# Attention with two accumulator banks, three banks for two units' scores, and a gate part moved ahead of the sample's

## The chip, the core and the metric

The kernel runs on one core of a Trainium2 chip. The metric is the device time of one launch in microseconds (us). The core's engines are TensorE (PE, with weight loads as PEld), VectorE (DVE), ScalarE (ACT), GpSimd (POOL) and SyncE (SP), which issues nearly all DMAs. TensorE writes its results to PSUM, which has eight banks of 512 float32 columns on 128 partitions.

## The reference

One layer step for a prompt of 2048 rows and a sample of 32 rows, each of 1024 columns:

```
z = rms_norm(x) @ w_in                       # 1024 -> 3072, split in six parts of 512
xl, gl, q, k, v, ga = split(z)
q, k = rms_norm per head (8 heads of 64)
lru = rg_lru(causal_conv(xl))                # gated linear recurrence over the rows
att = softmax(q k / 8 + bias[rel]) v         # each chunk of 64 rows reads itself and 8 chunks back
mix = concat(lru * silu(gl), att * silu(ga)) @ w_out
h   = x + mix
y   = h + (p @ w_pe) * sigmoid(rms_norm(h) @ w_pg)
```

The sample attends to 512 cached rows and its own 32. The outputs are y for prompt and sample, and the new states. Values are kept as pairs of float16 halves (high and low part), so one product of two matrices is three products of halves.

## The kernel before, in words

The rows are worked on in 16 tiles of 128 (tiles 0 to 15), and the sample is a seventeenth. A first stage, up to about 650 us, makes the projections and the recurrence and stores q, k, v and the gate path to memory. The second stage is attention, output projection and output gate, and the change lies there.

*Attention.* A tile is cut into units: one head each (eight to a tile; tile 1 has two heads in each of four units; the sample has four heads in each of two). Per unit, in this order:

- `u_scores`: TensorE multiplies q with two to ten blocks of keys (line L977, two matmuls of 128 columns for each block of 128 keys, ten matmuls for a unit from tile 4 on) into a score tile in PSUM, `pss`. VectorE adds the bias, takes the row's maximum and writes to SBUF (L988), and forms the exponent's offset (L991). ScalarE takes the exponential (L994).
- `u_split`, called after the next unit's scores: the high half is made by ScalarE (L1009, even units) or GpSimd (L1007, odd units), the low half by VectorE (L1010); both stand in `Phl`, of which there are three. SyncE issues a transposing DMA into `PT` (L1012), of which there are four.
- `u_pv`, five units later (`LAG`): TensorE multiplies the transposed probabilities with the values (L1032, 15 matmuls of 64 columns for a unit from tile 4 on) into the tile's accumulator in PSUM, `pso`.

After a tile's last unit `a_out` divides the accumulator by the sums into SBUF (VectorE, L1068), GpSimd multiplies with the gate path `ga` (L1069, which frees the buffer for the next `ga` load at L928), and `halves` splits and transposes the result (`An`, `AT`).

*Output.* `o_out` has four products of 12 matmuls for a tile into PSUM tiles `psu` (`L` is the recurrence's half, `AT` the attention's), each added to h by VectorE (L1112), and then a normalisation: ScalarE L1116, GpSimd L95 and L96, ScalarE L160, VectorE L163 writes `hn`, and SyncE transposes it to `hT` (L1121). `o_gate` multiplies `hT` with the gate's weights (`psg`, 24 matmuls) and p's halves with theirs (`pse`, 6), ScalarE (L1145, L1146) and VectorE (L1147) combine them, GpSimd (VectorE for tile 15) adds h (L1148), and SyncE stores (L1149). Tile 15's gate is cut into 512, 256 and 256 columns; others have two parts of 512. `o_load` loads the next tile's rows and transposes p (`pn`, `pT`). `psu`, `psg` and `pse` share three PSUM banks.

*Order.* A generator `fill` gives out the output work in portions: within a tile's time of eight units it alternates between the four products of one tile and the gate of the tile before it, one or two portions for each unit. For the sample it has its own list of portions. The program's text thus gives a priority, `flush_pv` (value product and `a_out`) gets a higher one, and a planner lays out each engine's queue ahead of time from its own estimates: it takes the work that it believes to be ready, in the order of priority. On the chip each queue runs in the order laid out, and waits at what is not there yet. The planner also places the semaphore waits, from which tile each instruction reads and writes.

*PSUM.* In this stage the scores have two tiles of 640 columns, each padded to two whole banks, the accumulator has one bank, and the output work three.

```
ps_s = pool("ps_s", bufs=2, space=PSUM)
ps_o = pool("ps_o", bufs=1, space=PSUM)
...
ps = ps_s.tile([128, 640], F32, tag="s", name="pss")
...
acc[i] = ps_o.tile([128, 512], F32, tag="o", name="pso")
```

Of the kernel before, what the change touches and what calls it, by code (L numbers as in the profile page):

```python
# [8 lines left out]
F32 = mybir.dt.float32  # L9
# [6 lines left out]
PSUM = bass.MemoryType.PSUM  # L16
# [18 lines left out]
def hybrid_layer(  # L35
# [853 lines left out]
    ch = pool("ch")  # L889
    ao = pool("ao")  # L890
    ol = pool("ol")
    ps_s = pool("ps_s", bufs=2, space=PSUM)
    ps_o = pool("ps_o", bufs=1, space=PSUM)
    units, acc, sums = {}, {}, {}
    kv, qT, sgT, nkv = {}, {}, {}, [0]

# [68 lines left out]
    def u_scores(i, u):  # L965

        ks = keys_of(i)
        ps = ps_s.tile([128, 640], F32, tag="s", name="pss")
        q = qT[i]
        parts, W, WP = unit_parts(i, u)  # L970
        for together in [parts] if i == SAMPLE else [[p] for p in parts]:
            for j, (key, n) in enumerate(ks):
                k = k_of(key)
                for a in range(2):
                    for h, R, rw, c0 in together:
                        c = slice(c0 + j * 128, c0 + j * 128 + n)
                        last_mm[0] = nc.tensor.matmul(ps[rw, c], lhsT=q[:, h % 2, a * 4 + h // 2, :R], rhs=k[:, h, :n],  # L977
                                         start=a == 0, stop=a == 1)
        m = 1 if i == SAMPLE else len(parts)
        mx = sm.tile([128, m], F32, tag=f"mx{m}", name="mx", bufs=3)  # L980
        if i == SAMPLE:
            S = biasS[u]
            nc.vector.scalar_tensor_tensor(S[:, :W], ps[:, :W], ratS, S[:, :W], op0=OP.mult, op1=OP.add)
            nc.vector.tensor_reduce(mx, S[:, :W], axis=AX.X, op=OP.max)
        else:
            S = T("S", [128, 640], F32, 3, ch)
            for j, (h, _, _, c0) in enumerate(parts):
                nc.vector.tensor_tensor_reduce(out=S[:, c0:c0 + W], in0=ps[:, c0:c0 + W], in1=bias[:, h, 640 - W:],  # L988
                                               op0=OP.add, op1=OP.max, scale=1.0, scalar=-3e38, accum_out=mx[:, j:j + 1])
        nb = sm.tile([128, m], F32, tag=f"nb{m}", name="nb", bufs=3)  # L990
        nc.vector.tensor_scalar(nb, mx, nscP, LN1024, op0=OP.mult, op1=OP.add)  # L991
        for j in range(m):
            e, c0 = (u, 0) if i == SAMPLE else parts[j][0::3]
            nc.scalar.activation(S[:, c0:c0 + W], S[:, c0:c0 + W], AF.Exp, bias=nb[:, j:j + 1], scale=scP,  # L994
                                 accum_out=sums[i][:, e:e + 1])
        units[i, u] = S
# [158 lines left out]
    def fill():  # L1155
        prev = iter(())
        for n, i in enumerate(order):
            o = o_out(i)
            if i == SAMPLE:

                for g, k in ((o, 4), (prev, 2), (o_gate(i), 4), (o, 1), (prev, 9)):
                    for _ in range(k):
                        if next(g, 0) != 0:
                            yield
                break
            for which in (0, 0, 1, 0, 1, 0, 1, 1):
                next(prev if which else o, None)
                yield
                if which == 0 and n + 1 < len(order) and S["o", i].get("hT") is None and not S.get(("o", order[n + 1])):
                    o_load(order[n + 1])  # L1170
            next(o, None)
            prev = o_gate(i)
        yield
# [15 lines left out]
    for n, (i, u) in enumerate(slots):  # L1189
# [14 lines left out]
        elif fl is None:  # L1204
            esr.close()
            wgp, ot = pool("wgp", side="right"), pool("ot", side="right")
            ps = pool("ps", bufs=3, space=PSUM, side="right")
# [93 lines left out]
```

## Time and profile before

| | |
|---|---|
| median of 3 runs | 1235.5 us (1233.63 to 1238.19) |
| the profiled execution | 1231.86 us, its span 1229.9 us |
| granted TensorE clock, mean | 0.947 |
| TensorE busy | 1078.4 us, 88% of the span |
| VectorE busy | 850.8 us, 69% |
| ScalarE busy | 591.3 us, 48% |
| GpSimd busy | 430.5 us, 35% |

The page that comes with a run shows one profiled execution. Times are counted from the span's start. A row of a group of instructions or of the timeline names line, engine, operation, what is written and read (out<-in) and how many instructions; in brackets stands the idle time of the engine before it and what ended that wait. Matmuls are pipelined, so those of one group overlap, and an engine whose queue stands still counts as idle.

### The profile page before, as it was taken

Reading aid. Unit: us, or ns where it says so; the run is one execution under the profiler, and the core shown is the slowest. Engines: PE = TensorE matmul, PEld = TensorE weight load, DVE = VectorE, ACT = ScalarE, POOL = GpSimd, SP = SyncE. Lnnn points to the kernel's source line nnn. Section 1 sums busy time; section 2 is a strip of 40 time slices with the busy share of each in tenths; the row PEclk is TensorE's granted clock in tenths of the full one; section 3 lists DMA queues with packets and bytes.
Section 4 is the critical chain, followed back from the end, with each engine's and each line's share of the span. In section 5 each row is a group of like instructions: output and inputs, shape, how many; then the busy total and the mean of one; then the engine's idle time right before and its main releaser. Section 6 shows DMA issues by size and latency. Waiting matters only on the chain. (4 is left out here: it accounts for less than half of the span.)

```text
span 1229.9 us, 22389 instructions
## 1 busy us (share of the span) xinstructions
PE 1078.4 (88%) x8395; PEld 626.2 (51%) x8395; DVE 850.8 (69%) x1932; ACT 591.3 (48%) x1040; POOL 430.5 (35%) x482
## 2 busy tenths in 40 slices
PE   3779997997697988788988699999999999999896
PEld 1335664653364654565644355555555555555443
DVE  5997557666885676877855676677777777677544
ACT  6542374544636746247654344444445444545223
POOL 3875123444542437452421222222222222222221
PEclk9789998998898998899899699999999999999998
DMA  8785225994856476540498987999989998998841
GB/s 288 212 216 159 75 67 143 263 253 127 228 159 172 143 204 180 167 107 22 146 338 262 239 156 162 171 207 194 191 186 198 181 196 190 185 200 188 187 84 26
DMA packets 357725, 217.47 MB, mean 177 GB/s; under 512 B 296032, under 2 KB 298632, under 8 KB 357488
## 3 DMA queue, kind: packets, MB, share of 16 engines
q1 hardware_dynamic: 357184, 215.50, 72.0%
q8 instruction: 65, 1.06, 0.4%
q10 hardware_dynamic: 432, 0.54, 0.1%
q14 instruction: 44, 0.36, 0.1%
HBM read 98.87 MB, written 46.76 MB: 118 GB/s over the span
## 5 line engine op out<-in xcount | busy, mean ns | idle before, releaser
L183 PE MATMUL psp<-wA,xT 128*128 128x512 f16 x1536 | 368.3, 400 | 30.1 <-ACT sq L656 9.9
L183 PEld LDWEIGHTS <-xT 128*128 128x128 f16 x1536 | 155.9, 102 | 264.2 <-issue 82.0
L994 ACT ACTIVATE S<-S,nb,s 128x640 f32<-128x640 f32 (+5 forms) x130 | 110.5, 850 | 221.4 <-DVE nb L991 211.8
L183 PE MATMUL psg<-g,hT 128*128 128x512 f16 (+1 forms) x792 | 179.8, 376 | 4.4 <-DMA hT<-hn 2.7
L587 PE MATMUL psx<-xT,wl 128*128 128x256 f16 x1536 | 178.7, 276 | 0.0
L587 PEld LDWEIGHTS <-wl 128*128 128x128 f16 x1728 | 157.3, 99 | 25.6 <-issue 2.1
L1010 DVE TENSOR_TENSOR Phl<-S,Phl 128x640 f16<-128x640 f32 (+4 forms) x126 | 96.9, 773 | 89.4 <-POOL Phl L1007 52.7
L1032 PE MATMUL pso<-kv,PT 128*128 128x64 f16 (+1 forms) x1704 | 116.9, 195 | 25.6 <-DMA PT<-Phl 13.2
L1032 PEld LDWEIGHTS <-PT 128*128 128x128 f16 (+2 forms) x1800 | 109.7, 99 | 47.5 <-issue 16.8
L1007 POOL TENSOR_SCALAR Phl<-S 128x640 f16<-128x640 f32 (+4 forms) x63 | 49.1, 779 | 213.7 <-ACT S L994 179.8
L183 PEld LDWEIGHTS <-hT 128*128 128x128 f16 x792 | 73.6, 98 | 79.8 <-DMA hT<-hn 3.4
L977 PE MATMUL pss<-kv,qT 128*128 128x128 f16 (+2 forms) x1200 | 107.0, 221 | 6.3 <-DVE mx L988 4.4
L977 PEld LDWEIGHTS <-qT 128*128 128x128 f16 (+1 forms) x1200 | 93.9, 99 | 19.6 <-issue 6.2
L988 DVE CUSTOM_DVE_ANT_0 S<-pss,bias 128x640 f32<-128x640 f32 (+4 forms) x128 | 93.0, 731 | 2.5 <-PE pss L977 2.0
L183 PE MATMUL psu<-o,AT 128*128 128x512 f16 x384 | 91.8, 390 | 1.3 <-DMA AT<-An 1.3
L183 PE MATMUL psu<-o,L 128*128 128x512 f16 x384 | 88.0, 379 | 0.0
L1148 POOL TENSOR_TENSOR gt<-gt,h 128x512 f32<-128x512 f32 (+1 forms) x32 | 41.7, 1304 | 60.7 <-DVE gt L1147 56.4
L95 POOL TENSOR_SCALAR fh<-ssqh,e 128x8 f32<-128x8 f32 (+1 forms) x34 | 17.5, 514 | 126.4 <-DVE ssqh L282 99.8
L96 POOL TENSOR_TENSOR fh<-fh,pw 128x8 f32<-128x8 f32 (+1 forms) x34 | 61.0, 1793 | 1.6
L183 PEld LDWEIGHTS <-AT 128*128 128x128 f16 x384 | 36.6, 101 | 43.5 <-issue 5.7
L183 PEld LDWEIGHTS <-L 128*128 128x128 f16 x384 | 35.6, 98 | 38.5
L90 PE MATMUL psm<-dg,ones 128*128 128x128 bf16 x25 | 6.0, 241 | 55.7 <-DVE dg L87 29.7
(284 smaller groups left out, 1693.5 us busy)
## 6 DMA issues: line engine op xcount, KB each, us to landing
stw<-in_w_in_dram SPq DMA_DIRECT2D x20, 512.0 KB, 7.1
x<-in_x_prompt_dram SPq DMA_DIRECT2D x16, 512.0 KB, 4.8
stg<-in_w_out_dram SPq DMA_DIRECT2D x16, 512.0 KB, 5.1
stg<-in_w_ple_gate_dram SPq DMA_DIRECT2D x16, 512.0 KB, 4.8
qT<-qd SPq DMA_DIRECT2D x32, 256.0 KB, 5.4
kv<-kvd SPq DMA_DIRECT2D x16, 512.0 KB, 4.1
h<-in_x_prompt_dram SPq DMA_DIRECT2D x16, 512.0 KB, 4.5
out_dram<-gt SPq DMA_DIRECT2D x31, 256.0 KB, 2.3
```

What stands on the lines that cost most here:

```text
L90: nc.tensor.matmul(ps, lhsT=ones, rhs=dg, start=True, stop=True)
L95: nc.gpsimd.tensor_scalar(dst, ssq, mul, add, op0=OP.mult, op1=OP.add)
L96: nc.gpsimd.tensor_tensor(dst, dst, pw[:R, :n], op=OP.pow)
L183: m = nc.tensor.matmul(ps[:R], lhsT=l(a), rhs=r(e), start=first and j == 0, stop=last and j == 2)
L587: m = nc.tensor.matmul(o, lhsT=wl[j][:, k, a, g * 128:(g + 1) * 128], rhs=rhs, start=i == 0, stop=i == 23)
L977: last_mm[0] = nc.tensor.matmul(ps[rw, c], lhsT=q[:, h % 2, a * 4 + h // 2, :R], rhs=k[:, h, :n], start=a == 0, stop=a == 1)
L988: nc.vector.tensor_tensor_reduce(out=S[:, c0:c0 + W], in0=ps[:, c0:c0 + W], in1=bias[:, h, 640 - W:], op0=OP.add, op1=OP.max, scale=1.0, s ...
L994: nc.scalar.activation(S[:, c0:c0 + W], S[:, c0:c0 + W], AF.Exp, bias=nb[:, j:j + 1], scale=scP, accum_out=sums[i][:, e:e + 1])
L1007: nc.gpsimd.tensor_scalar(v[:, 0, :W], P[:, :W], 1.0, 1.0, op0=OP.mult, op1=OP.mult)
L1010: nc.vector.tensor_tensor(v[:, 1, :W], P[:, :W], v[:, 0, :W], op=OP.subtract)
L1032: nc.tensor.matmul(o[rw, o0:o0 + HD], lhsT=t[:n, a * (WP // 128) + c0 // 128 + j, rw], rhs=v[:n, e, h * HD:h * HD + HD], start=first and m ...
L1148: (nc.vector if end else nc.gpsimd).tensor_tensor(gt[:R], gt[:R], s["h"][:R, c], op=OP.add)
```

## The change

The accumulator gets two banks, one for each of two successive tiles. The two score tiles become one tile of three banks, `ps3`, which is never given back: every second unit uses its first columns, the others its last. A unit of 640 columns then has 128 of them in the middle bank, and the matmuls of a second unit are issued in another order, so that its block in the middle bank comes last, as it does in a first unit. Units of at most 512 columns (tiles 0 to 3) do not touch the middle bank. In the sample's list of portions, tile 15's gate gives four portions (the 512 columns and the first 256) ahead of the sample's gate instead of two (the 512 columns).

```
-    ps_s = pool("ps_s", bufs=2, space=PSUM)
-    ps_o = pool("ps_o", bufs=1, space=PSUM)
+    ps_s = pool("ps_s", bufs=1, space=PSUM)
+    ps_o = pool("ps_o", bufs=2, space=PSUM)
+
+    ps3, nss = ps_s.tile([128, 1536], F32, name="ps3"), [0]
...
     def u_scores(i, u):
         ks = keys_of(i)
-        ps = ps_s.tile([128, 640], F32, tag="s", name="pss")
         q = qT[i]
         parts, W, WP = unit_parts(i, u)
+        second, nss[0] = nss[0] % 2, nss[0] + 1
+        ps = ps3[:, 1536 - WP:] if second else ps3[:, :WP]
+        blocks = list(enumerate(ks))
+        if second:
+            blocks = blocks[1:] + blocks[:1]
         for together in [parts] if i == SAMPLE else [[p] for p in parts]:
-            for j, (key, n) in enumerate(ks):
+            for j, (key, n) in blocks:
...
-                for g, k in ((o, 4), (prev, 2), (o_gate(i), 4), (o, 1), (prev, 9)):
+                for g, k in ((o, 4), (prev, 4), (o_gate(i), 4), (o, 1), (prev, 9)):
```

## Rows read from the trace of the kernel before

**Rows 1.** What TensorE waited for, 640 us on: total us, times, longest us.

```profile
PE pso L1032 <- DVE att L1068: 12.4, 12, 2.2
...
PE pss L977 <- DVE mx L988: 4.4, 6, 1.7
```

**Rows 2.** Busy time by stretch (tiles 6 to 14; tile 5), clock, DMA share, GB/s.

```profile
809.96:1105.63 295.67, 283.56 (x2773) 166.77 (x2772) 212.25 (x505) 138.88 (x244) 82.08 (x99) 1.00 0.95 193
778.33:809.96 31.63, 31.41 (x310) 18.50 (x309) 20.61 (x52) 13.88 (x25) 8.89 (x10) 1.00 0.91 173
```

**Rows 3.** All that VectorE waited for, 809.96 to 1105.63 us.

```profile
DVE Phl L1010 <- POOL Phl L1007: 34.8, 18, 2.1
DVE Phl L1010 <- ACT Phl L1009: 25.4, 27, 1.9
DVE pn L163 <- POOL pn L158: 14.6, 9, 2.7
DVE hn L163 <- ACT hn L160: 7.6, 9, 0.8
```

**Rows 4.** Timeline of TensorE in tile 13: start, us, what.

```profile
1043.54 0.22 PE L977 MATMUL pss<-kv,qT 128*128 128x128 f16 x1
...
1059.38 0.28 PE L1032 MATMUL pso<-kv,PT 128*128 128x64 f16 x4
...
1062.09 0.72 PE L977 MATMUL pss<-kv,qT 128*128 128x128 f16 x10
...
1065.72 0.60 PE L1032 MATMUL pso<-kv,PT 128*128 128x64 f16 x15 [1.62 <-DVE att L1068]
```

**Rows 5.** Timeline of VectorE, tile 13 to the next hn.

```profile
1045.05 0.81 DVE L988 CUSTOM_DVE_ANT_0 S<-pss,bias 128x640 f32<-128x640 f32 x1
...
1063.49 0.83 DVE L1010 TENSOR_TENSOR Phl<-S,Phl 128x640 f16<-128x640 f32 x1 [1.25 <-ACT Phl L1009]
1064.24 0.82 DVE L988 CUSTOM_DVE_ANT_0 S<-pss,bias 128x640 f32<-128x640 f32 x1
...
1064.98 0.69 DVE L1068 TENSOR_TENSOR att<-pso,fo 128x512 f32<-128x512 f32 x1
...
1066.63 1.48 DVE L163 SCALAR_TENSOR_TENSOR hn<-h,rs,hn 128x1024 f16<-128x1024 f32 x1 [0.84 <-ACT hn L160]
...
1077.28 1.47 DVE L163 SCALAR_TENSOR_TENSOR pn<-p,hr,pn 128x256 f16<-128x256 f32 x1 [2.66 <-POOL pn L158]
...
1099.94 1.47 DVE L163 SCALAR_TENSOR_TENSOR hn<-h,rs,hn 128x1024 f16<-128x1024 f32 x1 [0.84 <-ACT hn L160]
```

**Rows 6.** Timeline of SyncE's DMA issues from tile 13 on.

```profile
1062.97 1.37 SPq L1012 DMA_TRANSPOSE PT<-Phl  x1
1067.05 0.32 SPq L928 DMA_DIRECT2D ga<-gad  x1
1068.13 2.15 SPq L1121 DMA_TRANSPOSE hT<-hn  x1
1070.38 1.72 SPq L1012 DMA_TRANSPOSE PT<-Phl  x1
1072.19 1.36 SPq L1046 DMA_TRANSPOSE pT<-pn  x1
```

**Rows 7.** Timeline of GpSimd in the same lap.

```profile
1076.76 0.48 POOL L158 TENSOR_SCALAR pn<-p,hr 128x256 f16<-128x256 f32 x1 [4.46 <-DMA pT<-pn]
```

**Rows 8.** Timeline of TensorE at the kernel's end.

```profile
1203.49 1.46 PE L183 MATMUL pse<-wE,pT 128*128 128x512 f16 x6
1210.19 3.60 PE L181 MATMUL psg<-g,hT 128*32 128x512 f16 x24 [5.24 <-DMA hT<-hn]
...
1217.41 2.79 PE L183 MATMUL psg<-g,hT 128*128 128x256 f16 x24
```

**Rows 9.** Timeline of VectorE at the kernel's end: the last two adds of tile 15.

```profile
1224.28 0.42 DVE L1148 TENSOR_TENSOR gt<-gt,h 128x256 f32<-128x256 f32 x1
...
1226.69 0.42 DVE L1148 TENSOR_TENSOR gt<-gt,h 128x256 f32<-128x256 f32 x1
```

## The prediction

> **What bounds the kernel now.** The page's lines by slice show TensorE nearly full from the attention stage on, so I read the list of what TensorE waits for over that stage first [rows 1]. Two entries touch the change: the first value product of a tile waits 12.4 us in total (12 times) for VectorE's L1068, which empties the single accumulator; scores wait 4.4 us (6 times) for VectorE's L988, which empties a score buffer.
>
> The second view is the table by stretch [rows 2]. From the first scores of tile 6 to those of tile 15, nine laps of one tile each, 295.67 us pass and TensorE is busy 283.56: 32.85 us a lap, of which 31.5 are work. The lap before took 31.63 with almost no idle time. So at most 12.1 us can come out of these laps, and the DMA share is 0.95 in them.
>
> A wait of TensorE is worth something only if TensorE sets the lap, so the third view is what VectorE waited for in the same nine laps [rows 3]. TensorE is not in it. VectorE waits for the halves that GpSimd (34.8 us) and ScalarE (25.4) make, which in turn hang on VectorE's maxima, for pn (14.6) and for hn (7.6).
>
> The fourth reading is one lap in order of time, engine by engine. In tile 13 the last matmuls of tile 12's value products start at 1059.38 [rows 4]. TensorE goes on with other work, the ten scores at 1062.09 in it, then stands 1.62 us until L1068 lets it start tile 13's first value product at 1065.72. L1068 stands in VectorE's queue behind L1010 and L988, both late [rows 5]. What makes VectorE late is a loop without TensorE in it. The normalised rows hn start on VectorE at 1066.63 [rows 5]; SyncE issues their transpose at 1068.13, a transpose of probabilities at 1070.38 and the transpose of p at 1072.19 [rows 6]. GpSimd waits 4.46 us for that last one and starts pn at 1076.76 [rows 7]; VectorE's half of pn starts at 1077.28, and its queue, turn by turn with ScalarE and GpSimd as in [rows 3], comes to the next hn at 1099.94 [rows 5]. That lap is 33.31 us, and TensorE's 31.5 fit inside it. Taking TensorE's wait away by itself gives this loop nothing.
>
> **The change part by part.**
>
> *A second accumulator bank.* It removes the wait of a tile's first value product (15 matmuls, 0.60 us [rows 4]) for L1068. No instruction is added. What that product lets go is the point. The transposed probabilities have four buffers, so unit 4's transpose needs the buffer of unit 0, whose product ends at 1066.32 [rows 4]. Unit 4's halves are ready at 1064.32 (L1010, 1063.49 plus 0.83 [rows 5]). SyncE's queue is idle from 1064.34 to 1067.05, where the load of ga stands [rows 6]. But unit 4's transpose stands behind ga and hn's transpose, at 1070.38, and costs 1.72 us there and some 0.1 to the next issue, inside the loop. Without the wait the product runs with the scores from 1062.09 and is over about 1063.4, so the transpose (the one at 1062.97 took 1.37 us) fits into the idle 2.71 us. Whether it goes there is the planner's choice: the queue's order is laid out anew from its own estimates, and what held this transpose back there is the product behind L1068. If it moves, p's transpose and pn come 1.8 us earlier. VectorE's waits for pn are 14.6 us in nine laps [rows 3], 1.6 a lap, so that is what the loop can lose: 33 becomes 31.5, TensorE's own work. From above the nine laps thus give the 12.1 us of TensorE's idle time; from below, if the order stays, 0. I take the gain as likelier than not, since the old order fits a late product.
>
> *Three banks for two units' scores.* From tile 4 on a unit has 640 columns; one unit takes bank 0 and a fifth in bank 1, the next a fifth in bank 1 and bank 2. A matmul of the last block is now kept apart from the reading of the other unit in the same bank. Eight matmuls of ten wait for the unit before last, as they did; the last two wait for L988 of the unit just before. In tiles 0 to 3 units stay in banks 0 and 2, so what falls in them of the waits of [rows 1] for L988 stays. For the new wait: unit 1 of tile 13 starts its last block at 1043.54 [rows 4], and L988 of unit 0 runs from 1045.05 to 1045.86 [rows 5]. So TensorE would stand 2.3 us at that place, and the rest of that unit's value products, interleaved with the scores, and the gate products with it. Lower bound 0 (the lag of VectorE shrinks as its loop shortens, or the planner puts the block behind other work); upper bound 2.3 a lap, 20.7 in nine. Against the spare 1.3 a lap it can be wholly hidden while the loop stays at 33, but not once the loop is down to TensorE's work. I let it cost a third of the 12.1, some 4 us, nearer to the lower end: a stall moves all later matmuls, so the lags of later units shrink by it.
>
> The row says that VectorE reads a unit up to some 3 us after the next unit's scores; no row has two units in one bank. The Trainium skill, PSUM — Partial Sum Buffer, section "PSUM bank collisions raise a hardware error", says that two engines must be kept apart by bank and quadrant, not by address; by it the two last matmuls cannot pass L988 although their columns differ, and by the address alone the 4 us would be 0 and the sum 4 larger. No row of before shows it.
>
> *768 columns before the sample's gate.* Now TensorE ends the 512-column part of the last tile at 1204.95 and stands 5.24 us for the sample's hT [rows 8]. The two 256-column parts follow the sample's gate from 1217.41. One moves into the gap: 24 matmuls in 2.79 us and six more at about half of 1.46, an estimate of 3.5 in all, which fit. What is left behind the sample is one part, and it ends where the first of the two ends now: its last add runs from 1224.28 to 1224.70, the second's from 1226.69 to 1227.11 [rows 9]. That is 2.4 us; by TensorE alone it would be 3.5, and I take the smaller, since the outputs of the sample ahead of it may hold the first part's end. If the cover were gone, if the sample's hT came 3.5 us earlier, nothing would be gained.
>
> *Sum.* 12.1 less 4.1 is 8.0, plus 2.4: 10.4 us off. The profiled span of 1229.9 becomes 1219.5; that execution took 1231.86, and the median shown is 1235.5, 3.6 above it. I carry the difference over: 1235.5 less 10.4 is 1225.1.
>
> **The rivals.**
>
> *Only the tail pays.* SyncE's order stays, the loop stays at 33 us, and TensorE's freed time returns as waits for transposes or for L988. For it: VectorE never waits for TensorE in the nine laps, and the DMA engines are at 0.95. Against it: the transpose at 1070.38 is late by exactly the product that waited. 1235.5 less 2.4: 1233.1.
>
> *TensorE's waits come out whole.* The first value products' 12.4 us and 3.5 in the tail go, and the shared bank costs nothing: 1235.5 less 15.9 is 1219.6. For it: the laps' idle time is almost all this wait. Against it: the lag at 1043.54. The Trainium skill, Perfetto Trace Analysis, section "Matmuls", advises rotating independent groups through banks so that emptying one overlaps the next; by it this is the case. The trace shows the wait, but also the loop that hides its worth.
>
> *The shared bank makes it slower.* Each lap has the 2.3 us stall of unit 1, nothing shortens the loop, and the stall exceeds the idle time: 20.7 less 12.1 less 2.4 is 6.2 more, 1241.7. It decides once the stalls of a lap exceed TensorE's spare 1.3 us and VectorE's reads start moving with them. For it: the lag recurs in the lap; unit 6's ten scores end at 1062.81 [rows 4] and L988 of unit 5 at 1065.06 [rows 5], so the stall for L1068 that goes there may come back as one of 2.3. Against it: TensorE's delay shortens the lag it waits for, and the stalls need not add up.
>
> **How the numbers follow.** My case 0.42, the tail alone 0.28, all waits out 0.17, slower 0.13. What can be told from no change is about 0.5%, 6.2 us: 1229.3 to 1241.7. My case by itself spans 1221.0 (the bank costs nothing: 12.1 plus 2.4) to 1229.1 (it takes two thirds of the 12.1), below that bound with 0.41 of its 0.42; with the whole-waits case that is 0.58 faster. The slower case stands at the upper bound, and 0.08 of its 0.13 lie above it. The rest, 0.34, is the same. For 8 in 10 the range reaches from 1217, below the whole-waits case, to 1238, above the tail's case; the slower one's upper part is left out.
>
> **What the profile after would show.** Right: no entry for L1068 among TensorE's waits; unit 4's transpose ahead of hn's; laps of 31.5 to 32.2 us; a 256-column gate between the 512-column one and the sample's; the wait for hT down from 5.24 to some 1.7. A new entry would be scores waiting for L988 in tiles 5 to 15, 4 to 20 us in total. Wrong: laps still 32.8, with the transposes in their old order, means the tail alone; laps above 33 with scores waiting for L988, the slower case. The forecast fails if the planner reorders another queue, which no row can tell.

## The result and the profile after

The changed kernel took 1247.5 us (median of 6 runs, 1244.8 to 1251.6), the kernel before 1234.9 in the same runs: a ratio of 1.0097, 95% interval 1.0075 to 1.0119. It is slower by some 12 us where I forecast 10 less. The profiled execution took 1250.39 us with a span of 1248.4.

What TensorE waited for from 640 us on (us in total, times, longest) shows the wait that the change removes gone, and another in its place:

```profile
PE ps L983 <- DVE mx L994: 24.4, 20, 5.4
PE pso L1038 <- DMA PT<-Phl: 13.5, 7, 5.0
...
PE psg L181 <- DMA hT<-hn: 2.7, 1, 2.7
```

No entry is left for the accumulator, 12.4 us in [rows 1] (its VectorE line is now L1074). Scores waiting for the maximum (L994, before L988) grew from 4.4 us to 24.4.

By stretch, the nine laps from tile 6 to tile 15 and two pieces of tile 0 (the last numbers are the granted clock, the DMA share and GB/s):

```profile
659.61:667.62 8.01, 8.01 (x28) 3.14 (x26) 1.78 (x7) 4.81 (x9) 0.30 (x1) 0.66 0.90 296
...
681.94:687.28 5.34, 5.34 (x30) 2.51 (x29) 2.05 (x8) 1.59 (x6) 0.30 (x1) 1.00 0.27 77
...
831.72:1125.70 293.98, 283.07 (x2779) 167.33 (x2775) 214.23 (x506) 138.89 (x243) 81.91 (x99) 1.00 0.98 194
```

The laps became a little shorter, 32.66 us against 32.85 [rows 2]. So the loss lies ahead of them: tile 4's first scores start at 762.65 instead of 744.99 (17.7 later), tile 6's at 831.72 instead of 809.96 (21.8 later, so tiles 4 and 5 lose another 4.1, 3.3 of them in waits for the maximum). The nine laps give back 1.7; from tile 15 on it is 122.7 us instead of 124.2. In sum the span is 18.5 longer; the medians lie 12.7 apart, so a part of the 18.5 belongs to the two executions that were profiled.

Where it is lost shows in TensorE's timeline in tile 0 of the kernel after (start, us, what, idle time before it and what ended it):

```profile
641.06 0.28 PE L983 MATMUL ps<-kv,qT 128*128 128x128 f16 x2
645.99 7.97 PE L183 MATMUL psp<-wA,xT 128*128 128x512 f16 x24 [4.65 <-ACT t L325]
...
659.45 0.37 PE L983 MATMUL ps<-kv,qT 128*128 128x128 f16 x2 [5.43 <-DVE mx L994]
659.61 8.01 PE L183 MATMUL psp<-wA,xT 128*128 128x512 f16 x24
...
672.72 0.64 PE L1038 MATMUL pso<-kv,PT 128*128 128x64 f16 x6 [4.98 <-DMA PT<-Phl]
...
673.36 7.96 PE L183 MATMUL psp<-wA,xT 128*128 128x512 f16 x24
...
681.94 5.34 PE L183 MATMUL psp<-wA,xT 128*128 128x512 f16 x24
```

The same piece of the kernel before:

```profile
643.75 8.05 PE L183 MATMUL psp<-wA,xT 128*128 128x512 f16 x24 [4.85 <-ACT t L325]
...
652.25 0.27 PE L977 MATMUL pss<-kv,qT 128*128 128x128 f16 x2 [0.27 <-DVE mbL L91]
652.36 5.34 PE L183 MATMUL psp<-wA,xT 128*128 128x512 f16 x24
...
665.03 5.34 PE L183 MATMUL psp<-wA,xT 128*128 128x512 f16 x24
```

The three projections (L183, 24 matmuls each) that the code puts behind the scores of units 1, 3 and 5 end at 670.37 before and at 687.28 after, 16.9 us later. The terms: the projection ahead of them starts 2.2 later (643.75 before, and 641.33 to 644.62 in seven other runs with the score tiles of before, so this term need not be the change's); unit 1's scores stand 5.43 us for the maximum of unit 0; the three take 21.3 us instead of 16.0, two of them at a granted clock of 0.66 to 0.67 (between the levels of 1.2 and 2.4 GHz) after TensorE stood for some 5 us, where before they ran at 1.00; and 4.98 us pass for a transpose that before was waited for later, at 688.08. Less two waits of before in this piece (1.65 and 0.27) that is 16.0.

Why the maximum is late, VectorE's timeline of after tells:

```profile
658.50 0.69 DVE L322 SCALAR_TENSOR_TENSOR vTo<-psp,vTo 128x512 f16<-128x512 f32 x1 [1.11 <-ACT vTo L321]
659.11 0.28 DVE L994 CUSTOM_DVE_ANT_0 S<-ps,bias 128x128 f32<-128x128 f32 x1
659.31 0.08 DVE L994 DVE_READ_ACCUMULATOR2_ANT mx<- 128x1 f32 x1
```

Unit 0's scores were done at 641.3, but its maximum stands in VectorE's queue behind the last of the stage before, until 659.11. Unit 1's scores start 0.06 us after the read of its accumulator has ended. Unit 0 lies in bank 0 and unit 1 in bank 2; they share no bank. In the program as built, the first score product of every unit of tiles 0 to 15 waits for the count that VectorE's counter has after the maximum of the unit just before (the first: 992; the next: 995, 999, 1002), wherever the two lie in the tile of 1536 columns. The layer that places the waits treats any two uses of that PSUM tile as overlapping. Three banks in one tile are one buffer here.

In the nine laps the same wait stands once a tile, 0.74 to 1.89 us, and takes the place of the one for the accumulator. The first row here is all that TensorE waits for in these laps after, the second the main one before:

```profile
PE ps L983 <- DVE mx L994: 10.9, 9, 1.9
...
PE pso L1032 <- DVE att L1068: 11.1, 9, 2.2
```

VectorE's waits there after:

```profile
DVE Phl L1016 <- ACT Phl L1015: 27.1, 28, 1.4
DVE Phl L1016 <- POOL Phl L1013: 23.0, 18, 2.0
DVE pn L163 <- POOL pn L158: 10.7, 9, 1.8
DVE fo L1073 <- ACT S L1000: 9.7, 9, 1.1
```

Against [rows 3], pn costs 3.9 us less and the halves 10.1 less, but fo is new with 9.7. SyncE's queue, an order of [rows 6], is laid out anew (tile 12):

```profile
1045.83 3.05 SPq L1127 DMA_TRANSPOSE hT<-hn  x1
1048.98 1.35 SPq L1018 DMA_TRANSPOSE PT<-Phl  x1
1050.43 1.36 SPq L1052 DMA_TRANSPOSE pT<-pn  x1
1051.88 1.27 SPq L1052 DMA_TRANSPOSE AT<-An  x1
```

One transpose of probabilities still stands between those of hn and of p, as in [rows 6], but it is unit 3's, and unit 4's comes behind p's: unit 4 went back, not forward as I had forecast.

The end went as forecast (TensorE, to be laid beside [rows 8]):

```profile
1225.11 2.78 PE L183 MATMUL psg<-g,hT 128*128 128x256 f16 x24
...
1231.26 3.30 PE L181 MATMUL psg<-g,hT 128*32 128x512 f16 x24 [2.72 <-DMA hT<-hn]
...
1238.02 2.79 PE L183 MATMUL psg<-g,hT 128*128 128x256 f16 x24
```

A 256-column part stands in the gap and the wait for hT is 2.72 instead of 5.24. From the end of the 512-column part to the end of the span it is 23.13 us instead of 24.95.

### The profile page after: what moved, and what is told of

Its sections match the earlier page's. It is cut to its first block, busy times and chain, and to the rows that moved or that the text cites. A ratio compares the mean times of both kernels' runs of the same rounds, so it can differ in the third digit from the quotient of the medians.

```text
span 1248.4 us, 22357 instructions
## 1 busy us (share of the span) xinstructions
PE 1084.2 (87%) x8395; PEld 627.9 (50%) x8395; DVE 856.6 (69%) x1932; ACT 592.2 (47%) x1040; POOL 427.5 (34%) x482
## 5 line engine op out<-in xcount | busy, mean ns | idle before, releaser
L183 PE MATMUL psp<-wA,xT 128*128 128x512 f16 x1536 | 373.0, 403 | 33.7 <-ACT sq L656 10.0
L183 PEld LDWEIGHTS <-xT 128*128 128x128 f16 x1536 | 156.8, 103 | 270.1 <-issue 89.1
L183 PE MATMUL psg<-g,hT 128*128 128x512 f16 (+1 forms) x792 | 179.0, 376 | 2.5 <-DMA hT<-hn 1.4
L183 PEld LDWEIGHTS <-hT 128*128 128x128 f16 x792 | 74.0, 99 | 80.1 <-DMA hT<-hn 3.2
L983 PE MATMUL ps<-kv,qT 128*128 128x128 f16 (+2 forms) x1200 | 86.3, 221 | 27.7 <-DVE mx L994 24.4
L994 DVE CUSTOM_DVE_ANT_0 S<-ps,bias 128x640 f32<-128x640 f32 (+4 forms) x128 | 93.3, 731 | 22.2 <-PE ps L983 22.2
L1038 PE MATMUL pso<-kv,PT 128*128 128x64 f16 (+1 forms) x1704 | 86.8, 195 | 13.7 <-DMA PT<-Phl 13.5
L1038 PEld LDWEIGHTS <-PT 128*128 128x128 f16 (+2 forms) x1800 | 75.9, 100 | 44.4 <-DMA PT<-Phl 19.6
L183 PE MATMUL psu<-o,AT 128*128 128x512 f16 x384 | 90.8, 385 | 0.4 <-DMA AT<-An 0.4
L183 PE MATMUL psu<-o,L 128*128 128x512 f16 x384 | 90.6, 386 | 0.0
L983 PEld LDWEIGHTS <-qT 128*128 128x128 f16 (+1 forms) x1200 | 69.3, 99 | 35.8 <-issue 32.0
L1118 DVE SCALAR_TENSOR_TENSOR h<-psu,cA,h 128x512 f32<-128x512 f32 x64 | 47.6, 743 | 15.9 <-PE psu L183 15.7
L183 PEld LDWEIGHTS <-AT 128*128 128x128 f16 x384 | 36.0, 99 | 40.4 <-issue 3.4
L183 PEld LDWEIGHTS <-L 128*128 128x128 f16 x384 | 36.1, 99 | 39.8 <-issue 2.8
```

The costliest lines, as they stand in the source:

```text
L183: m = nc.tensor.matmul(ps[:R], lhsT=l(a), rhs=r(e), start=first and j == 0, stop=last and j == 2)
L1038: nc.tensor.matmul(o[rw, o0:o0 + HD], lhsT=t[:n, a * (WP // 128) + c0 // 128 + j, rw], rhs=v[:n, e, h * HD:h * HD + HD], start=first and m ...
L1118: nc.vector.scalar_tensor_tensor(h[:R, c], pt[:R], cA[:R, j, half:half + 1], h[:R, c], op0=OP.mult, op1=OP.add)
```

## The experiments

The table has each run's ratio to the kernel before on the same chip, and from its profile the start of tile 4's and tile 6's first scores, the nine laps from there to tile 15's, and the rest. One profile is one execution: in some of them TensorE ran a lap at a mean clock of 0.95, which lengthens its work in that lap by some 2 us, so a difference of 2 to 4 us between nine laps says little. Nor does attention start at the same time in each: from the projection that stands at 643.75 before to tile 4's first scores it is 101.2 us before, 99.5 to 104.0 in seven other runs with its score tiles, 116.7 after, 116.2 in e1, 114.1 in e2, 102.6 in e4, 108.7 in e8 and 94.2 in e5. By this measure the change loses 15.4 us up to tile 4, not 17.7.

| run | ratio (interval) | tile 4 | tile 6 | nine laps | rest |
|---|---|---|---|---|---|
| before | 1 | 744.99 | 809.96 | 295.67 | 124.2 |
| after | 1.0097 (1.0075 to 1.0119) | 762.65 | 831.72 | 293.98 | 122.7 |
| e1 scores only | 1.0152 (1.0131 to 1.0173) | 760.76 | 830.90 | 294.58 | 122.9 |
| e2 one buffer | 1.0107 (1.0091 to 1.0122) | 760.38 | 829.15 | 295.77 | 117.4 |
| e3 tail only | 0.9974 (0.9957 to 0.9991) | 741.61 | 806.20 | 299.22 | 123.5 |
| e4 early own tiles | 1.0089 (1.0073 to 1.0106) | 746.59 | 815.49 | 301.79 | 122.6 |
| e5 three tiles | 0.9989 (0.9969 to 1.0008) | 739.34 | 811.91 | 293.90 | 121.7 |
| e6 two accumulators, two outputs | 1.0053 (1.0032 to 1.0074) | 735.12 | 810.39 | 295.63 | 131.1 |
| e7 one accumulator, two outputs | 1.0037 (1.0013 to 1.0061) | 744.86 | 809.77 | 294.44 | 130.7 |
| e8 free projections | 1.0052 (1.0030 to 1.0073) | 751.17 | 817.81 | 294.84 | 121.8 |
| e9 less TensorE work | 1.0009 (0.9991 to 1.0026) | 746.56 | 805.79 | 300.79 | 127.5 |
| e10 fewer loads | 0.9935 (0.9912 to 0.9957) | 742.94 | 807.53 | 289.25 | 123.9 |
| e11 halves on ScalarE | 1.0036 (1.0018 to 1.0054) | 745.36 | 809.95 | 302.80 | 123.4 |
| e12 two pn | 0.9973 (0.9953 to 0.9993) | 742.76 | 807.93 | 297.08 | 124.5 |
| e13 two pn, tail | 0.9943 (0.9919 to 0.9966) | 743.00 | 807.90 | 292.09 | 119.8 |
| e14 two pn, three tiles | 0.9967 (0.9947 to 0.9986) | 737.52 | 810.54 | 290.30 | 120.3 |
| e15 nb on ScalarE | 1.0191 (1.0168 to 1.0213) | 750.12 | 815.03 | 304.50 | 131.2 |
| e16 the same, all opened | 1.0114 (1.0095 to 1.0133) | 748.18 | 821.71 | 300.70 | 124.0 |
| e17 five PT, tail | 0.9805 (0.9784 to 0.9827) | 743.88 | 808.47 | 281.48 | 116.9 |
| e18 fewer loads, all opened | 0.9843 (0.9815 to 0.9871) | 740.34 | 811.58 | 281.68 | 121.7 |

### Which part loses, and where

**e1, the scores alone.** From the kernel after:

```diff
-    ps_o = pool("ps_o", bufs=2, space=PSUM)
+    ps_o = pool("ps_o", bufs=1, space=PSUM)
...
-                for g, k in ((o, 4), (prev, 4), (o_gate(i), 4), (o, 1), (prev, 9)):
+                for g, k in ((o, 4), (prev, 2), (o_gate(i), 4), (o, 1), (prev, 9)):
```

> The score part alone: one tile of three banks for the scores as in the changed kernel, but one accumulator bank and 256 columns ahead of the sample as before. Theory one, mine: in the built program the first score product of every unit waits for the maximum (L994) of the unit just before, wherever in the three banks it writes, so the three banks act as one buffer; in tiles 0 to 3 that holds up the three projections queued behind scores. Then this part alone carries the loss: the first scores of tile 4 at about 762 us as in the changed kernel (before: 745), the laps from tile 6 to 15 no better than before's 32.85, and 1249 to 1256 us in all. Theory two: the loss came with the second accumulator, whose order was laid out anew; then the time is that of before within 0.5%, 1229 to 1241.

Measured 1250.4 us, tile 4 at 760.76, laps of 32.73. The score part alone carries the loss; theory two, by which the second accumulator does, falls. Without the accumulator's second bank and the tail it is slower by another half per cent; the tail is 0.26% of that (e3), and what is left for the bank lies within the intervals.

**e2, one plain buffer.** From the kernel before:

```diff
-    ps_s = pool("ps_s", bufs=2, space=PSUM)
-    ps_o = pool("ps_o", bufs=1, space=PSUM)
+    ps_s = pool("ps_s", bufs=1, space=PSUM)
+    ps_o = pool("ps_o", bufs=2, space=PSUM)
...
-                for g, k in ((o, 4), (prev, 2), (o_gate(i), 4), (o, 1), (prev, 9)):
+                for g, k in ((o, 4), (prev, 4), (o_gate(i), 4), (o, 1), (prev, 9)):
```

> The scores get one plain buffer of 640 columns, no third bank and no sharing; second accumulator and 768 columns as in the changed kernel. Theory one: three banks that act as one buffer cannot be told from one buffer, so the time is that of the changed kernel within 0.5% (1241 to 1254 us), with the first scores of tile 4 near 762 us. Rival, the shared middle bank costs by itself or the separate outer banks still give overlap: then this run is slower than the changed kernel by more than 0.5% (rival: two buffers in part) or faster by as much (rival: the sharing costs).

Measured 1245.3 us, tile 4 at 760.38, and scores waiting 24.4 us, 20 times, the longest 5.4: the very numbers of after. Three banks in one tile are worth what one buffer of two banks is.

**e3, the tail alone.** From the kernel before, (prev, 2) becomes (prev, 4).

> Only the tail's move on the kernel before: four steps of the last tile's gate ahead of the sample's instead of two. From the traces of before and after, where the stretch from the end of the 512-column part to the end went from 24.95 to 23.13 us, I expect 1.8 us less, a ratio of 0.9985 (0.997 to 1.000), with the wait for the sample's hT down from 5.24 to about 2.7. If the tail's move had part in the loss, the ratio would be over 1.002.

Measured 0.9974, 3.2 us by the ratio: the part pays, with an interval that holds the forecast 2.4.

**e4, own tiles for tiles 0 to 3.** From the kernel after:

```diff
+    ps_e = pool("ps_e", bufs=3, space=PSUM, stack=early)
...
-        ps = ps3[:, 1536 - WP:] if second else ps3[:, :WP]
+        if WP <= 512 and i != SAMPLE:
+            ps = ps_e.tile([128, 512], F32, tag="s", name="pss")
+        else:
+            if not wide:
+                early.close()
+                wide.append(pool("ps_s", bufs=1, space=PSUM).tile([128, 1536], F32, name="ps3"))
+            ps = wide[0][:, 1536 - WP:] if second else wide[0][:, :WP]
```

> The changed kernel, but units of at most 512 columns (tiles 0 to 3) take their scores in one-bank tiles of their own, three of them; the three shared banks are opened at tile 4. Theory one: scores and the projections queued behind them no longer wait for the maximum just before, so the start of tile 4 comes back from 762 to about 745 us, and the laps and tail keep what the change gave there (1.7 and 1.8 us): 1226 to 1233 us in all, at or a little below before. Rival, the loss is of the laps or of the planner's other reorderings: then tile 4 starts near 762 still, and the time stays above 1243.

The ramp up to tile 4 is back, tile 4 at 746.59 against 762.65; the time is not, 1242.7 us. From tile 4 to 15 it takes 370.7 us, against 360.6 before and 363.1 after, so my expectation that the laps keep their small gain was wrong. Scores wait 16.6 us there for the maximum just before (19 times), after 14.2 (13 times), and two of the laps ran at a mean clock of 0.95, some 3.5 us. Together that is most of the 7.6 us by which it is longer than after, but no run shows that the wait, and not another order of the queues, makes it so.

**e8, projections let loose.** From the kernel after, the line `with tc.issue_after(last_mm[0].ins):` is taken away.

> The changed kernel, but the three projections in tile 0 are not put behind the scores of units 1, 3 and 5; the planner may place them freely. Theory one: the ramp's loss comes by these projections, which stand 5.4 us behind scores that wait for L994 and then run at the lower clock (8.0 instead of 5.3 us); free of them they fill the waits, and at least half of the 17.7 us comes back: 1233 to 1240 us. Rival: the scores' own chain from L994 to scores to L994 sets the ramp, whatever stands beside it; then within 0.5% of the changed kernel.

Tile 4 starts at 751.17, 11.5 us earlier, and 1238.3 us in all. But 3.5 of the 11.5 stand already at the projection ahead (642.46 against 645.99); counted from there 8.0 of the 15.4 us are back and 7.5 are left. So the order behind the scores makes about half of the wait's price in the ramp.

**e5, the sharing as it was described.** From the kernel after, the score tile becomes three:

```diff
+    ps_s = pool("ps_s", bufs=2, space=PSUM)
+    ps_m = pool("ps_m", bufs=1, space=PSUM)
+    mid, nss = ps_m.tile([128, 256], F32, name="mid"), [0]
...
+        pw = ps_s.tile([128, 512], F32, tag="s", name="pss")
+        pm = mid[:, second * 128:second * 128 + 128]
...
+                if W > 512:
+                    nc.vector.tensor_tensor_reduce(out=S[:, 512:], in0=pm, in1=bias[:, h, 512:], op0=OP.add, op1=OP.max,
+                                                   scale=1.0, scalar=mx[:, j:j + 1], accum_out=mx[:, j:j + 1])
```

> The sharing as it was described: three score tiles of one bank each, two outer ones in turn and one for the fifth block of both units; VectorE takes a unit of 640 columns in two instructions (512, then 128), so that only the two products of the fifth block wait for the unit just before. Second accumulator and tail as in the changed kernel. Theory one: nothing waits wholly for the unit just before, so tile 4 starts near 745 us and the ramp's 17.7 us are back; VectorE pays some 0.3 us a unit (2.4 a lap, an estimate from the 0.08 us accumulator read and a fifth of L988's 0.81) inside its loop, so laps of 32.5 to 34; 1227 to 1240 us. Rival, the banks themselves collide (products into the middle bank or beside it are slowed): then TensorE's busy time per lap rises above 31.5 us. Second rival, the loss is the second accumulator's: tile 4 starts near 762 still.

Measured 1229.0 us; the loss is gone, and with it all that the change was to bring: 0.9989, the tail alone gave 0.9974. TensorE's waits in the nine laps are one row:

```profile
PE mid L983 <- DVE mx L999: 8.4, 12, 1.9
```

That is the stall of the last two products that the prediction had put at 4 us. Unit 4's transpose stands ahead of hn's in every lap here, as forecast, and the wait for the accumulator is gone, yet the laps are 32.66 us, not 31.5. TensorE's busy time is 284.75 in the nine laps against 283.56, so a third bank beside a read costs nothing to speak of. VectorE's second instruction takes 0.34 us and 0.08 for its accumulator; it is busy 224.30 us instead of 212.25, and the laps did not lengthen. What they would be without these 12 us of VectorE no run shows.

### What the second accumulator is worth

**e6 and e7** are a pair: whole score buffers (three of one bank for tiles 0 to 3, then two of two), two output tiles instead of three, and two accumulators (e6, whose diff stands here) or one (e7, without the first two lines).

```diff
-    ps_o = pool("ps_o", bufs=1, space=PSUM)
+    ps_o = pool("ps_o", bufs=2, space=PSUM)
...
-            ps = pool("ps", bufs=3, space=PSUM, side="right")
+            ps = pool("ps", bufs=2, space=PSUM, side="right")
```

> Whole score buffers, two of two banks from tile 4 on (three of one bank in tiles 0 to 3), and two accumulators; the eighth bank comes from the output tiles, two instead of three. To be read against the next run, which differs in one accumulator alone. If the second accumulator is worth what the prediction said, this run's laps are 31.5 to 32.2 us and it is 8 to 12 us faster than the next run; if the loop of the other engines sets the lap whatever TensorE does, the two are within 4 us.

> The control of the run before it: one accumulator, two output tiles, the same score buffers. What it loses against the kernel before is the price of the third output tile; I expect 0 to 12 us, since gate and products of weights use three in turn. Its waits show the first value product of a tile behind L1068 again, some 1.3 us a lap.

1238.4 and 1236.7 us, 295.63 and 294.44 in the nine laps: the second accumulator is worth nothing there. But the pair does not price the wait that it was to remove. My expectation that e7 shows this wait again missed. In e7's nine laps TensorE waits for the two output tiles,

```profile
PE psu L183 <- ACT gt L1152: 8.4, 9, 1.5
PE psg L183 <- DVE h L1119: 2.4, 3, 0.9
```

and for nothing else. What the pair does show is the moved transpose. In e6 that of unit 4 stands ahead of hn's in every lap, as forecast (SyncE's queue in tile 12):

```profile
1034.18 2.23 SPq L1019 DMA_TRANSPOSE PT<-Phl  x1
1036.46 2.73 SPq L1128 DMA_TRANSPOSE hT<-hn  x1
1039.29 1.21 SPq L1053 DMA_TRANSPOSE pT<-pn  x1
```

Over eight laps from tile 7 on, the time from hn on VectorE to pn on GpSimd fell from 9.1 (e7) to 8.7 us, not by 1.6, since hn's transpose now waits behind the moved one (from the start of hn to it 2.55 us instead of 1.50), and pn to the next hn grew from 23.7 to 24.2. e7 also shows what the third output tile is worth: some 6 us in the end of the profiled execution (130.7 against 124.2), 4.6 by the ratio.

**e9, less work for TensorE.** From the kernel before, half of the weight products on L are left out (two of the four blocks of L's columns), so the output is not the reference's.

```diff
-                for k in range(4):
+                n = 2 if j else 4
+                for k in range(n):
...
```

> The kernel before, with half of the weight products on L left out (12 of a tile's matmuls of 512 columns, about 2.75 us of TensorE's 31.4 a lap); the output is not the reference's. What sets the lap of 32.85 us between tiles 6 and 15? If the loop of VectorE, ScalarE, GpSimd and SyncE, as the prediction had it, laps stay at 32.3 to 33.0 and TensorE's idle time grows to some 4 us a lap. If TensorE's own work with one stall that cannot be avoided, laps fall by 2.5 to 2.8, to about 30.2, and the time by 35 us or more.

The ratio is 1.0009, in the nine laps:

```profile
805.79:1106.58 300.79, 269.26 (x2666) 159.31 (x2665) 212.49 (x506) 135.95 (x244) 82.02 (x99) 0.98 0.94 190
```

TensorE is idle 31.5 us there, 3.5 a lap, and the laps are no shorter; four of them ran at a mean clock of 0.95, but the five at 1.00 are of 33.0 us in the mean. So TensorE's work does not set them. The run does not take away the wait for the accumulator, which is 18.2 us there: it shows that time of TensorE is worth nothing by itself, not what a value product is worth that starts earlier.

### What sets the lap

**e10, fewer loads.** From the kernel before; kv, for which the lines stand here, and qT and L likewise.

```diff
+        if not isinstance(key, tuple) and key != SAMPLE and key > 4:
+            kv[key] = kv[key - 5]
+            return
...
```

> The kernel before, with the loads of kv, qT and L left out from tile 5 on (older tiles are read again), 1.25 MB of the 6.3 MB that the queues move in a lap; the output is not the reference's. If the DMA engines, busy at 0.95 in the laps, set the lap, it falls from 32.85 to 31.5, TensorE's work; if not, laps stay within 0.3 us of 32.85 and the DMA share falls to about 0.85.

289.25 us, 32.14 a lap, half of the way to TensorE's work; the first three laps are of 31.3 us with no idle time, then stalls return. With fewer loads the transposes of probabilities land sooner (from issue to landing 4.6 us in the median before, 3.6 here), but that is not the whole.

**e11, upper halves all on ScalarE**: `if u % 2 and i == SAMPLE` in place of `if u % 2`.

> The kernel before, with the upper halves of every unit made by ScalarE, where odd units of the prompt's tiles had them from GpSimd. In the laps VectorE waits 34.8 us for GpSimd's halves and 25.4 for ScalarE's, and ScalarE is busy 139 of 296 us. If the loop through VectorE sets the lap, GpSimd's 0.9 us become some 0.7 and one hand-over goes in every second unit: laps of 31.5 to 32.3 instead of 32.85, 1220 to 1232 us. If something else sets it, the time is within 0.5% of before. If ScalarE becomes the late one (four more operations a lap, about 3 us), laps rise over 33.

Slower by 0.4%: VectorE's wait for GpSimd turns into one for ScalarE. The last of the three expectations.

**e12, e13, e14, a second pn buffer**, which opens the loop of the prediction where GpSimd waits for the transpose of p: alone, with the tail's move, and with e5.

```diff
-        n = T(f"{tag}n", [128, 2 * W], F16, 1, p)
+        n = T(f"{tag}n", [128, 2 * W], F16, 2 if tag == "p" else 1, p)
```

> The kernel before with a second buffer for pn, so that GpSimd need not wait for the transpose of the tile before's p. If the loop through that buffer sets the lap, GpSimd's wait for pT goes, VectorE's wait for pn (14.6 us in nine laps) with it, and laps fall from 32.85 to between 31.5 (TensorE's work) and 32.3: 1219 to 1229 us. If the lap is set by the order that VectorE's queue has by itself, or by the transposes on the DMA engines, laps stay within 0.3 us of 32.85 and the time within 0.5%.

> As the run before it, with the tail's move, which alone gave a ratio of 0.9974: 2 to 3 us below that run.

> Second pn buffer, the three score tiles, two accumulators, the tail's move. If the pn loop was what hid the second accumulator's worth, laps come down to 31.5 to 32.0 and the time to 1215 to 1224 us, below the run with the tail alone. If not, the time is that of the three tiles without the second pn buffer, 1229, within 0.5%.

VectorE's waits in the nine laps of e12:

```profile
DVE Phl L1010 <- POOL Phl L1007: 37.5, 27, 2.3
DVE Phl L1010 <- ACT Phl L1009: 35.0, 27, 3.9
DVE hn L163 <- ACT hn L160: 7.6, 9, 0.8
```

The wait for pn is gone, 14.6 us of [rows 3], and the wait for halves has grown from 60.2 to 72.5. The time from hn to pn (taken as above, over the same eight laps) fell from 9.2 to 5.65 us, and the rest of the lap grew from 23.8 to 27.3: the same sum. The loop through pn, my account of the lap, did not set it. The ratios, 0.9973, 0.9943 and 0.9967, are small gains; e13 is 3.7 us below e12 by the medians, and e14's laps are of 32.26 us, so the loop through pn was not what hid the worth of the second accumulator either.

**e15, e16, nb on ScalarE**, alone and with e14: in VectorE's queue nb of a unit stands behind L1010 of the unit before.

```diff
...
-        nc.vector.tensor_scalar(nb, mx, nscP, LN1024, op0=OP.mult, op1=OP.add)
+        nc.scalar.activation(nb, mx, AF.Identity, bias=lnT, scale=nscP)
```

> The kernel before, with nb made by ScalarE from the maximum, instead of by VectorE (0.2 us each, eight a lap). If the chain from unit to unit through VectorE's queue (nb behind L1010, L1010 behind the half, the half behind the exponential, that behind nb) sets the lap, ScalarE's 141 us of waiting for nb and VectorE's 60 us of waiting for halves shrink, and laps fall from 32.85 to 31.5 to 32.2 us: 1218 to 1227 us. If it does not, laps stay at 32.6 to 33.0 and the time within 0.5%; ScalarE's eight small operations a lap cost nothing, since it waits half of the time.

> nb on ScalarE with the second pn buffer, the three score tiles, two accumulators and the tail's move (e14 with nb moved). If the chain through nb was the last that held the laps, TensorE stands no longer in them: 31.4 to 31.7 us a lap, 1213 to 1221 us. If the DMA engines with their transposes hold them, laps stay at e14's 32.3 with VectorE waiting less for halves and more, or ScalarE and GpSimd, for buffers that a transpose has not read yet.

A miss, 1.9% and 1.1% slower. In e15 tile 4 starts 5.1 us later, the nine laps are 8.8 longer and the rest 7.0. nb takes 0.39 us on ScalarE where VectorE took 0.21, and the queues are laid out in another order (the maximum, L988, stands where nb had stood, behind L1010); which of the two costs the time is not shown. The pair tells nothing against that chain and nothing for it.

**e17, a fifth buffer for transposed probabilities**, with the tail's move, from the kernel before:

```diff
-        t = T("PT", [128, 10, 128], F16, 4, ch)
+        t = T("PT", [128, 10, 128], F16, 5, ch)
```

> The kernel before with the tail's move and a fifth buffer for transposed probabilities. If SyncE's queue, held by the value products that free these buffers, sets the lap, laps fall from 32.85 to 32.2 or less and the time is 4 to 10 us below that of the tail alone (1229): 1219 to 1225 us. If not, within 3 us of the tail alone.

1208.6 us, a ratio of 0.9805, where the tail's move alone gave 0.9974: faster than both kernels, with one accumulator and the old score buffers. The nine laps and the rest:

```profile
808.47:1089.95 281.48, 281.48 (x2773) 166.75 (x2772) 213.82 (x505) 139.13 (x243) 86.06 (x100) 1.00 1.00 202
1089.95:1206.88 116.93, 103.21 (x1001) 55.37 (x999) 67.81 (x139) 41.25 (x69) 26.56 (x34) 0.98 0.57 125
```

TensorE is busy in every microsecond of 31.28 a lap. It waits in these laps neither for L1068 nor for L988, without a bank more; ahead of them 5.1 us of waits for L988 are left. Unit 4's transpose stands ahead of hn's here too. Of the 23.0 us between the spans 14.2 are won in the nine laps and 7.3 behind them. What VectorE waits for in the nine laps has changed with it:

```profile
DVE Phl L1010 <- POOL Phl L1007: 36.8, 18, 2.5
DVE Phl L1010 <- ACT Phl L1009: 15.6, 26, 1.3
DVE hn L163 <- ACT hn L160: 7.8, 9, 1.0
DVE h L1112 <- PE psu L183: 3.9, 5, 1.2
DVE pn L163 <- POOL pn L158: 1.8, 2, 0.9
```

And two rows of what SyncE's queue waits for in e17:

```profile
SPq L1012 <- DVE Phl L1010: 39.4, 33, 2.0
SPq L1012 <- PE pso L1032: 29.0, 28, 2.2
```

In the nine laps of the kernel before, SyncE's transposes of probabilities seldom waited for their own data:

```profile
SPq L1012 <- PE psu L183: 14.0, 11, 2.5
SPq L1012 <- PE pso L1032: 13.9, 9, 2.4
SPq L1012 <- PE psg L183: 12.5, 6, 2.4
...
SPq L1012 <- DVE Phl L1010: 5.3, 8, 0.8
```

There 50.1 us of these waits end with TensorE (these rows and those for pse, 5.3, and pss, 4.4) and 5.3 with the halves; with a fifth buffer 39.4 end with the halves. But 45.5 still end with TensorE there (the second row, and 16.5 for pss, pse, psu and psg), so these waits by themselves do not tell what set the lap; the run does. My reading of both is that with four buffers a transpose had to wait for a value product four units back, and everything behind it in SyncE's queue with it.

**e18, e14 with fewer loads.** What e10 leaves out, left out of e14.

> The three score tiles, two accumulators, second pn buffer and tail of e14, without the loads of kv, qT and L from tile 5 on; the output is not the reference's. e14's laps are 32.26 us. If what is left of TensorE's idle time there is the DMA engines' doing, laps fall to 31.4 to 31.7, as in the first laps of e10, and the time to 1211 to 1220. If it is the order of VectorE's queue, laps stay at 32.0 to 32.4.

```profile
811.58:1093.26 281.68, 281.65 (x2774) 166.82 (x2772) 225.63 (x651) 140.51 (x243) 80.58 (x100) 1.00 0.84 161
```

TensorE is full here too, with four PT buffers. The transposes of probabilities land in 3.8 us in the median, against 4.5 in e14, so that transposes that land sooner do what one more buffer does is the likely reading; but they take 3.8 in e17 too, with all loads, and no run changes the landing alone. e17 has TensorE full at a DMA share of 1.00, so the share by itself was no bound.

## Why the prediction was wrong

**The step that failed** is the one on the three banks: "Eight matmuls of ten wait for the unit before last, as they did; the last two wait for L988 of the unit just before", and with it "In tiles 0 to 3 units stay in banks 0 and 2, so what falls in them of the waits of [rows 1] for L988 stays." All ten wait for the unit just before, in every tile of the prompt (e2 has the same waits; e5, with tiles of their own, has not). I took disjoint columns and disjoint banks for enough; what the wait goes by is the tile, and the change had made two tiles one. That cost 15.4 us up to tile 4 (17.7 by the clock of the two profiles), in a stretch for which I had quoted no row, because I had looked for the change's price only where it shares a bank. That the planner goes by tiles I had written down myself, and not used.

**The rival on that side** had the right engine pair and sign, and the wrong place: 20.7 us in nine laps, by the shared bank. Measured are 10.9 us of waits in the laps, which stand where the 11.1 us for the accumulator stood, and the rest in the ramp, where projections are tied behind the scores (e8) and run at a lower clock after the stall (0.66 to 0.67).

**The 12.1 us of the laps** was the second failure. In the kernel after nothing came of them, since another wait of the same length stood in their place. But e5 has neither the accumulator's wait nor the old place of unit 4's transpose, and won 0.2 us a lap, not 1.3. The prediction said rightly that TensorE's time is worth nothing by itself (e9), and [rows 3] were read rightly. It then took the loop of hn, pT, pn and VectorE for the pace and gave it 1.6 us a lap from a moved transpose. Where the transpose moved (e6), hn to pn gained 0.4 us; and opening that loop wholly (e12) left the sum of its legs at 33.0. The sentence "The transposed probabilities have four buffers, so unit 4's transpose needs the buffer of unit 0" named the resource that frees the lap when there is one more (e17), and the prediction went past it to the accumulator.

The Trainium skill, Perfetto Trace Analysis, section "Matmuls", by which rotating groups through banks lets emptying overlap, stood for the case that all waits come out. No run here shows that rotation worth anything for the accumulator: 32.66 us a lap in e5, 32.85 in e6 and 32.72 in e7, its control. None shows it alone either, since e5 adds work to VectorE and e7's laps have no wait for the accumulator to remove.

**The 4 us for the shared bank**: e5 shows 8.4 us of waits for the middle tile in nine laps, twice the 4, in laps that are no longer than before. No run here shows whether the bank itself, not the tile, would have forced them.

**The tail** was right: one part in the gap, hT's wait 2.72 (forecast 1.7), and 1.8 us off in the profile (forecast 2.4). With the tail alone (e3) they are 1.94 and 2.6, and 3.2 by the ratio.

**What stays open.** That one buffer more among the transposed probabilities frees the laps is shown; which link was the last to close the loop with four (the issue in SyncE's queue, the three buffers of Phl, or VectorE behind the halves) is argued from the waits, not shown. Nor is shown what a second accumulator is worth with two whole score buffers and three output tiles: that is nine banks of eight. Beside a fifth PT buffer it was not tried; with TensorE full in e17's laps nothing is left for it there.

## What to carry to other kernels

Before you count on two halves of one PSUM tile as two buffers, find out what a wait goes by: here it went by the tile, and the program's waits at the first use tell it. A wait on the busiest engine is a symptom until taking work off that engine moves the lap; e9's kind of run, work left out, tells it. Then follow what a queue's waits hang on to the buffer with the fewest copies, and try one more: 2.5 KB a partition for a fifth PT took the ratio from 0.9974 (e3) to 0.9805, and for a second accumulator bank no run shows a gain clear of noise.

## What the runs showed of the hardware

After TensorE stood some 5 us in tile 0, a projection took 8.01 us at a mean granted clock of 0.66, against 5.34 at 1.00: that stall cost its own length and half of a projection. The DMA engines at a mean share of 1.00 (202 GB/s) kept TensorE without a wait in e17's laps: a share of one was no sign of a bound there. An activation on one column per partition took 0.39 us on ScalarE, a tensor_scalar of it 0.21 on VectorE.
